# Seven block products for eight in half of the K range of 42 pairs of transposed units, with the attention heads kept in DRAM until pooling

## Chip, cores and metric

The kernel runs on one core of one Trainium2 chip. The metric is the time of one execution on the device in microseconds (us); lower is better. TensorE (PE) multiplies, VectorE (DVE) and ScalarE (ACT) work on tiles, GpSimd (POOL) has a few reductions and DMA issues, and SyncE (SP) issues nearly all DMAs.

## The reference

The input `x` is 512 rows of 2048 float32 values. Two layers follow each other. Each norms its rows, multiplies them with a wide input matrix, mixes the columns, and multiplies 2048 mixed columns with an output matrix:

```python
def even_mixer(h, w_in, pool_w, pool_scale, w_out, cos, sin):
    z = h @ w_in                                   # 1024 a_in, 1024 a_gate, 3 x 3072 q k v, 1024 b_gate
    a_in, a_gate, q, k, v, b_gate = jnp.split(z, _split_points(EVEN_COLS), axis=-1)
    ya = causal_pool_mixer(a_in, pool_w, pool_scale) * jax.nn.silu(a_gate)
    yb = dilated_attention(q, k, v, cos, sin) * jax.nn.silu(b_gate)
    return jnp.concatenate([ya, yb], axis=-1) @ w_out

def odd_mixer(h, w_in, ...):
    z = h @ w_in                                   # six groups of 1024 columns
    u, v, c_gate, d_val, d_glu, d_gate = jnp.split(z, _split_points(ODD_COLS), axis=-1)
    yc = chunked_sgu(u, v, ...) * jax.nn.silu(c_gate)
    d = d_val * jax.nn.sigmoid(d_glu)
    d = jax.nn.silu(layernorm(causal_depthwise_conv(d, ...), ...))
    yd = d * jax.nn.silu(d_gate)
    return jnp.concatenate([yc, yd], axis=-1) @ w_out
```

Attention has eight heads of 128 columns, each the softmax mixture of three dilated groups, with rotation of the first 32 columns of q and k.

## The kernel before

The normed rows stand transposed in SBUF in two parts, `Ah` and `Al` (128 partitions, 16 K tiles of 128, 512 tokens each), whose sum is the float32 value. A weight chunk is 128 x 1024 float32, 512 KB. SP loads it into `wraw` (three buffers); ACT copies it into the high part `whi` (L64), DVE takes the rest into the low part `wlo` (L65); there are three buffers of each part. Every product of a weight tile and a K tile is three matmuls: low weights with `Ah`, high weights with `Al`, high weights with `Ah`.

A *transposed unit* (`zt_item`, L125) makes 128 output columns for all 512 tokens in one PSUM bank: two chunks of 8 K tiles, 48 matmuls of 128x512 (L137 to L139). A *natural item* (`nat_item`, L146) makes rows of tokens by columns (L162 to L164), with 512 columns too; V, both output projections and the odd layer's V are of this kind.

The order of the even layer is: V for heads 0 to 3, 28 units (per head q and k of three groups, and the gate), V for heads 4 to 7, 28 units, then 16 pooling units with two small products (`mix_item`), then the output projection. The odd layer has four natural items, 24 units for the convolution's and the SGU's inputs (with the convolution's taps on DVE beside them, L681), 16 gate units, and the output projection.

When a head's last unit is done, `attention` (L430) starts: scores on PE (L445, L457), maximum over the groups (a POOL reduction, L474), subtraction (L479 to L483), exp on ACT (L481, L484), sums (L468 to L472), a second POOL reduction, a reciprocal (L503), while PE multiplies the exps with V (`oa`, `ob`, L490 to L497); two products (L504, L505) leave the gated head in `Y[:, 8 + h]`. A scheduler that follows the program's order fixes the order on each engine; engines then run their own lists in order and wait on semaphores. Pooling takes its tiles `xp`, `pa`, `pb` from the memory that the attention's tiles leave free (L569, L573).

Of the kernel before, what the change touches and what calls it, by code (L numbers as in the profile page):

```python
# [19 lines left out]
P = 128  # L20
D = 2048
# [13 lines left out]
P_END = 64 + 8 * TAPS  # L35


class Weights:
    """Streams the weight chunks in the order of use and splits each into two float32r parts."""

    def __init__(self, nc, raw_pool, split_pool, chunks, raw_bufs, ahead):
        self.nc, self.raw_pool, self.split_pool, self.chunks = nc, raw_pool, split_pool, chunks
        self.raw_bufs, self.ahead = raw_bufs, ahead
        self.raw, self.parts = [], []
# [12 lines left out]
    def split(self, upto):  # L57
        while len(self.parts) < min(upto, len(self.chunks)):
            i = len(self.parts)
            self.load(i + 1)  # L60
            hi = self.split_pool.tile([P, 1024], FR, tag="whi", name=f"whi{i}")
            lo = self.split_pool.tile([P, 1024], FR, tag="wlo", name=f"wlo{i}")
            for c in ((slice(0, 512), slice(512, 1024)) if i == 0 else (slice(0, 1024),)):
                self.nc.scalar.activation(hi[:, c], self.raw[i][:, c], AF.Copy)  # L64
                self.nc.vector.tensor_tensor(lo[:, c], self.raw[i][:, c], hi[:, c].bitcast(F32), op=OP.subtract)  # L65
            self.parts.append((hi, lo))

    def get(self, i):
        self.split(i + 1)
        self.load(i + 1 + self.raw_bufs)  # L70
        self.split(i + 1 + self.ahead)
        self.load(i + 1 + self.ahead + self.raw_bufs)
        return self.parts[i]


@with_exitstack
def trunk(ctx: ExitStack, tc: tile.TileContext, x, xt, out, ewv, ewz, ewo, epw, epost,
# [4 lines left out]
    raw_pool = ctx.enter_context(tc.tile_pool(name="raw_pool", bufs=3))  # L82
    split_pool = ctx.enter_context(tc.tile_pool(name="split_pool", bufs=3))
    xpool = ctx.enter_context(tc.tile_pool(name="xpool", bufs=2))
    small = ctx.enter_context(tc.tile_pool(name="small", bufs=2))
    dpool = ctx.enter_context(tc.tile_pool(name="dpool", bufs=1, space=bass.MemoryType.DRAM))
    psz = ctx.enter_context(tc.tile_pool(name="psz", bufs=4, space=bass.MemoryType.PSUM))
# [9 lines left out]
    x1d = dpool.tile([S, D], F32, name="x1d")  # L97

# [12 lines left out]

    def rsqrt_of(ssq, n, name):
# [7 lines left out]
    items = []  # L120

    def add_item(chunks, pe, after=None):
        items.append((chunks, pe, after))

    def zt_item(wz, u, after, order=(0, 1), mid=None):  # L125
        state = {}

        def pe(ci, hi, lo):
# [11 lines left out]
            if mid is not None:  # L140
                mid(ci)

        add_item([wz[u, :, 8 * o:8 * o + 8, :].rearrange("p k c -> p (k c)") for o in order], pe,
                 lambda: after(state["ps"]))

    def nat_item(wv, c, tts, after, perm=False, order=range(8), stagger=False):  # L146
# [36 lines left out]
        add_item([wv[c, :, 2 * o:2 * o + 2, :].rearrange("p k c -> p (k c)") for o in order], pe)  # L183
# [17 lines left out]
    def run_items(w, pos):  # L201
        for chunks, pe, after in items:
            for ci in range(len(chunks)):
                hi, lo = w.get(pos)
                pe(ci, hi, lo)
                done.append(pos)
                pos += 1
                if after is not None and ci == len(chunks) - 1:
                    after()
                step()  # L210
        items.clear()
        return pos

# [22 lines left out]
    first = {}  # L236

    def first_loads(i, t, chunk):
# [13 lines left out]
        if 2 <= i <= 5:  # L252
            xr = xpool.tile([P, D], F32, tag="xr", name=f"xn{i}")
# [32 lines left out]

    def load_rows(half, layer, rows):
        src = x if layer == 0 else x1d
        for tt in (2 * half, 2 * half + 1):
            if layer == 1 and half == 1:  # L290
                xr = od["V"][:, 2 * (tt - 2):2 * (tt - 1), :].rearrange("p a b -> p (a b)")
            else:
                xr = xpool.tile([P, D], F32, tag="xr", name=f"xr{layer}_{tt}")
# [87 lines left out]
    # ================= start =================  # L381
# [8 lines left out]
    # ================= even layer, attention =================  # L390
# [19 lines left out]

    def qk_after(g, qk, key):
        def after(ps):
            t = att.tile([P, S], F32, tag="qk", name=f"qk_{len(done)}", bufs=8)
            cos, sin = rp[:, 0, :], rp[:, 1, :]
            sw = att.tile([32, S], F32, tag="sw", name=f"sw_{len(done)}")
            if g == 0:
                nc.scalar.activation(t, ps, AF.Copy)
# [3 lines left out]
            else:  # L421
                nc.scalar.activation(perm_out(t), perm_in(ps), AF.Copy)  # L422
# [4 lines left out]
            qk[key] = t  # L427
        return after

    def attention(h, qk):  # L430
# [67 lines left out]
        y = Y[:, 8 + h, :]  # L498
# [6 lines left out]
        nc.vector.tensor_tensor(y, y, oas, op=OP.mult)  # L505
        yield 1

    def bgate_after(h, qk):
        def after(ps):
            nc.scalar.activation(Y[:, 8 + h, :], ps, AF.Silu)  # L510
            start(attention(h, qk))
        return after

    chunk_list = []
    w = Weights(nc, raw_pool, split_pool, chunk_list, 3, 2)
# [381 lines left out]
```

## Time and profile before

| | before |
|---|---|
| median of 3 runs | 2072.93 us (2072.93 to 2073.49) |
| the profiled execution: span from first to last instruction | 2071.4 us |
| PE busy, share of the span | 2055.5 us, 99% |
| DVE busy | 1156.7 us, 56% |
| ACT busy | 647.1 us, 31% |
| DMA, mean over the span | 117 GB/s |

The span leaves out what comes before the first and after the last instruction, so 1.5 us lie around it. A busy PE need not be a PE at its peak: matmuls are pipelined, so the distance from the start of one to the start of the next is the price of one, and the length of its record is not.

### The profile page before, as it was taken

How to read it: one execution, taken by the hardware profiler on the slowest of the kernel's cores; microseconds unless marked ns; L12 is line 12 of the kernel's file. 1: busy time of each engine (PE TensorE's matmuls, PEld its weight loads, DVE VectorE, ACT ScalarE, POOL GpSimd, SP SyncE). 2: the span in 40 equal slices, each digit the busy share in tenths (PEclk: the TensorE clock that was granted, in tenths of full speed). 3: DMA queues.
4: the chain of work that ended last, by engine and by line, in shares of the span. 5: the costliest groups of instructions: out<-in, count | busy, mean ns of one | idle time of the engine just before them, and what ended most of it. 6: DMA issues, size and time to landing. Idle time of an engine off the chain costs nothing.

```text
span 2071.4 us, 22339 instructions
## 1 busy us (share of the span) xinstructions
PE 2055.5 (99%) x9064; PEld 1699.7 (82%) x9064; DVE 1156.7 (56%) x1385; ACT 647.1 (31%) x793; POOL 87.4 (4%) x86
## 2 busy tenths in 40 slices
PE   8999999999999999999999999999999999999998
PEld 8988888889988888888888888888888888888886
DVE  4725656555224656566542435775889996324255
ACT  6422222323222322223332324553122223323243
POOL 1000101000000101001000000100000001000002
PEclk9999999999999999999999999999999999999999
DMA  8332222232322222222223337864222222223465
GB/s 299 92 101 89 94 83 82 86 98 82 92 92 92 89 85 91 82 92 82 92 93 101 112 97 222 281 216 155 87 92 92 97 97 92 92 91 122 133 211 196
DMA packets 68472, 241.78 MB, mean 117 GB/s; under 512 B 7792, under 2 KB 8048, under 8 KB 67088
## 3 DMA queue, kind: packets, MB, share of 16 engines
q1 hardware_dynamic: 67152, 234.05, 35.0%
q0 software_dynamic: 1216, 6.29, 0.8%
q8 instruction: 71, 1.16, 0.2%
q14 instruction: 33, 0.27, 0.0%
HBM read 231.93 MB, written 8.39 MB: 116 GB/s over the span
## 4 chain that ended last, share of the span: by engine, by line
PE 97%; DMA 1%; DVE 1%; ACT 0%; issue 0%; POOL 0%; SPq 0%; DVEq 0%; ACTq 0%; POOLq 0%
PE z L138 20%; PE z L137 20%; PE z L139 20%; PE n L162 11%; PE n L163 11%; PE n L164 11%; PE sg L457 1%; DMA wraw<-in_owv_dram 0%; DVE Y L313 0%; PE ob L497 0%; PE ob L496 0%; PE oa L490 0%; PE sgu L640 0%; PE sa L445 0%; PE tr L222 0%; DMA wraw<-in_owo_dram 0%
## 5 line engine op out<-in xcount | busy, mean ns | idle before, releaser
L65 DVE TENSOR_TENSOR wlo<-wraw,whi 128x1024 fp32r<-128x1024 f32 (+1 forms) x403 | 504.1, 1251 | 571.3 <-ACT whi L64 570.6
L137 PE MATMUL z<-Ah,wlo 128*128 128x512 f32 x1792 | 710.5, 396 | 0.0
L138 PE MATMUL z<-Al,whi 128*128 128x512 f32 x1792 | 708.8, 396 | 0.0
L64 ACT ACTIVATE whi<-wraw 128x1024 fp32r<-128x1024 f32 (+1 forms) x403 | 425.5, 1056 | 906.9 <-PE z L139 463.8
L139 PE MATMUL z<-Ah,whi 128*128 128x512 f32 x1792 | 708.7, 395 | 0.0
L163 PE MATMUL n<-wlo,Ah 128*128 128x512 f32 x1024 | 406.8, 397 | 0.3 <-DVE wlo L65 0.2
L164 PE MATMUL n<-whi,Ah 128*128 128x512 f32 x1024 | 405.5, 397 | 0.0
L139 PEld LDWEIGHTS z<-Ah,whi 128*128 128x128 f32 x1792 | 336.6, 188 | 81.0
L137 PEld LDWEIGHTS z<-Ah,wlo 128*128 128x128 f32 x1792 | 336.7, 188 | 80.6
L138 PEld LDWEIGHTS z<-Al,whi 128*128 128x128 f32 x1792 | 336.7, 188 | 80.6
L162 PE MATMUL n<-whi,Al 128*128 128x512 f32 x1024 | 392.3, 398 | 6.7 <-DVE Al L263 6.7
L162 PEld LDWEIGHTS n<-whi,Al 128*128 128x128 f32 x1024 | 223.2, 218 | 41.6 <-DVE Al L263 6.7
L163 PEld LDWEIGHTS n<-wlo,Ah 128*128 128x128 f32 x1024 | 223.4, 218 | 36.3 <-DVE wlo L65 1.3
L164 PEld LDWEIGHTS n<-whi,Ah 128*128 128x128 f32 x1024 | 223.3, 218 | 35.0
L681 DVE SCALAR_TENSOR_TENSOR Y<-dp,pc,Y 128x512 f32<-128x512 f32 x240 | 174.3, 749 | 3.6
L423 DVE LOAD_MASK_SELECT sw<-qk x32 | 0.4, 14 | 125.4 <-ACT qk L422 125.4
L422 ACT ACTIVATE qk<-z 128x512 f32<-128x512 f32 x32 | 19.1, 597 | 145.3 <-PE z L139 145.3
L474 POOL PARTITION_ALL_REDUCE mw<-mv x8 | 14.3, 1784 | 798.9 <-DVE mv L472 798.9
L424 DVE TENSOR_TENSOR sw<-sw,rp 32x512 f32<-32x512 f32 x32 | 34.3, 1071 | 1.1
L425 DVE TENSOR_TENSOR qk<-qk,rp 32x512 f32<-32x512 f32 x32 | 34.0, 1063 | 0.0
L426 DVE TENSOR_TENSOR qk<-qk,sw 32x512 f32<-32x512 f32 x48 | 32.3, 673 | 0.2
L735 DVE TENSOR_TENSOR Y<-Y,og 128x512 f32<-128x512 f32 x16 | 11.1, 691 | 38.0 <-ACT og L734 38.0
(153 smaller groups left out, 908.1 us busy)
## 6 DMA issues: line engine op xcount, KB each, us to landing
wraw<-in_ewz_dram SPq DMA_DIRECT2D x144, 512.0 KB, 3.7
wraw<-in_owz_dram SPq DMA_DIRECT2D x80, 512.0 KB, 3.8
wraw<-in_ewo_dram SPq DMA_DIRECT2D x48, 512.0 KB, 4.2
wraw<-in_owo_dram SPq DMA_DIRECT2D x48, 512.0 KB, 3.9
wraw<-in_ewv_dram SPq DMA_DIRECT2D x47, 512.0 KB, 3.6
wraw<-in_owv_dram SPq DMA_DIRECT2D x32, 512.0 KB, 3.8
xn<-in_x_dram SPq DMA_DIRECT2D x4, 1024.0 KB, 8.7
xr<-in_x_dram SPq DMA_DIRECT2D x16, 256.0 KB, 5.1
```

What stands on the lines that cost most here:

```text
L64: self.nc.scalar.activation(hi[:, c], self.raw[i][:, c], AF.Copy)
L65: self.nc.vector.tensor_tensor(lo[:, c], self.raw[i][:, c], hi[:, c].bitcast(F32), op=OP.subtract)
L137: nc.tensor.matmul(ps, wl[:, j], Ah[:, k, :], start=first, stop=False)
L138: nc.tensor.matmul(ps, wh[:, j], Al[:, k, :], start=False, stop=False)
L139: nc.tensor.matmul(ps, wh[:, j], Ah[:, k, :], start=False, stop=last)
L162: nc.tensor.matmul(ps, tok(Al, k, t), wh[:, j], start=first, stop=False)
L163: nc.tensor.matmul(ps, tok(Ah, k, t), wl[:, j], start=False, stop=False)
L164: state["mm"] = nc.tensor.matmul(ps, tok(Ah, k, t), wh[:, j], start=False, stop=last).ins
L424: nc.vector.tensor_tensor(perm_out(sw), perm_out(sw), perm_in(sin), op=OP.mult)
L425: nc.vector.tensor_tensor(perm_out(t[0:32, :]), perm_out(t[0:32, :]), perm_in(cos), op=OP.mult)
L426: nc.vector.tensor_tensor(t[0:32, :], t[0:32, :], sw, op=OP.add)
L681: nc.vector.scalar_tensor_tensor(acc, dp[:, k:k + S], wk, acc, op0=OP.mult, op1=OP.add)
```

## The change

For 42 pairs (u, v) of units (24 pairs of q and k, 4 of two heads' gates, 7 of pooling units, 7 of odd gate units) K tiles 0 to 7 are multiplied as before. For K tiles 8 to 15 the weights of both units and the activations are taken as 2 x 2 blocks: weights by unit and by half of the K range (tiles 8 to 11, and 12 to 15), activations by half of the K range and by half of the tokens. The eight block products of the plain form become seven (a Strassen form), each 4 K tiles by 256 tokens by three matmuls, 12 matmuls of 128x256. The sums of weight blocks are made on DVE in the raw buffers (L78) and then split (L69, L70); the sums of activation blocks, `S1` to `S4`, are made once per layer by `make_forms` (L191, L195). The sums of results are made by ACT copies of 256 columns out of PSUM (L294) and DVE additions (L297, L330) into a destination in SBUF.

Weights now have four raw and four split buffers. Part i of the split weights is made only once part i-4 has been used up, and raw load i only once raw buffer i-4 is released; the first weight chunk of a pair is released by the pair's last part. A head's gated result goes to DRAM (`ybd`, L741, a DMA from POOL's queue), and is read back into `Y` before pooling (L1067, on SP's queue). The scheduler's order follows from all this.

```diff
+RAW_BUFS, SPLIT_BUFS = 4, 4
...
+    def pair(self, ap, bp):
+        a, b = self.chunk(ap), self.chunk(bp)
+        L, R = slice(0, 512), slice(512, 1024)
+        def tt(out, x, y):
+            self.nc.vector.tensor_tensor(out, x, y, op=OP.subtract)
+        def f0(hi, lo):
+            self.split(hi, lo, self.raw[a])
+        def f1(hi, lo):
+            ra, rb = self.raw[a], self.raw[b]
+            tt(ra[:, L], rb[:, L], ra[:, L])
+            self.split(hi[:, L], lo[:, L], ra[:, L])
+            self.split(hi[:, R], lo[:, R], rb[:, R])
+        def f2(hi, lo):
+            ra, rb = self.raw[a], self.raw[b]
+            tt(rb[:, L], rb[:, R], rb[:, L])
+            tt(rb[:, R], rb[:, R], ra[:, L])
+            tt(ra[:, R], ra[:, R], rb[:, R])
+            self.split(hi, lo, rb)
+        def f3(hi, lo):
+            self.split(hi[:, L], lo[:, L], self.raw[a][:, R])
+        return [(self.part, ([a], f0, [])), (self.part, ([a, b], f1, [])),
+                (self.part, ([b], f2, [b])), (self.part, ([a], f3, [a]))]
     def load(self, upto):
         while len(self.raw) < min(upto, len(self.chunks)):
             i = len(self.raw)
+            if i >= self.raw_bufs and not self.raw_done[i - self.raw_bufs]:
+                return
...
+    def pump(self):
+        while True:
+            self.load(len(self.chunks))
             i = len(self.parts)
-            self.load(i + 1)
+            if i == len(self.specs) or (i >= self.split_bufs and not self.done[i - self.split_bufs]):
+                return
+            needs, make, frees = self.specs[i]
+            if any(r >= len(self.raw) for r in needs):
+                return
             hi = self.split_pool.tile([P, 1024], FR, tag="whi", name=f"whi{i}")
             lo = self.split_pool.tile([P, 1024], FR, tag="wlo", name=f"wlo{i}")
-            for c in ((slice(0, 512), slice(512, 1024)) if i == 0 else (slice(0, 1024),)):
-                self.nc.scalar.activation(hi[:, c], self.raw[i][:, c], AF.Copy)
-                self.nc.vector.tensor_tensor(lo[:, c], self.raw[i][:, c], hi[:, c].bitcast(F32), op=OP.subtract)
+            make(hi, lo)
+            for r in frees:
+                self.raw_done[r] = True
...
+    ybd = dpool.tile([8, P, S], F32, name="ybd")
...
+    def make_forms(layer, full, temps):
+        for i, n in enumerate(("S1", "S2", "S3", "S4")):
+            t = rpool.tile([P, 2, 4, 256], FR, tag=f"r{i}", name=f"{n}_{layer}")
+            FORMS[n] = (t[:, 0], t[:, 1])
...
+        for half in range(2):
+            ta, tb, tc_ = temps
+            a21, a22 = full(2, 1, half, ta), full(2, 2, half, tb)
+            tt(tb, a21, a22, OP.add)
+            split("S1", tb, half)
+            a11 = full(1, 1, half, tc_)
+            tt(ta, a11, a21, OP.subtract)
+            split("S3", ta, half)
+            yield 1
+            tt(tb, tb, a11, OP.subtract)
+            split("S2", tb, half)
+            a12 = full(1, 2, half, tc_)
+            tt(tc_, a12, tb, OP.subtract)
+            split("S4", tc_, half)
...
+    def pair_item(wz, u, v, dst_u, dst_v, after_u, after_v):
+        st = {}
+        ZL, XL = slice(0, 256), slice(256, 512)
+        L, Rt = slice(0, 512), slice(512, 1024)
+        makers = w.pair(chunk_of(wz, u, 1), chunk_of(wz, v, 1))
+        def made(i):
+            f, args = makers[i]
+            return f(*args)
+        def product(bank, where, hi, lo, name, start=False):
+            fh, fl = FORMS[name]
+            wh = hi.rearrange("p (k c) -> p k c", c=P)
+            wl = lo.rearrange("p (k c) -> p k c", c=P)
+            out = st[bank][:, where]
+            for j in range(4):
+                nc.tensor.matmul(out, wl[:, j], fh[:, j, :], start=start and j == 0, stop=False, skip_group_check=True)
+                nc.tensor.matmul(out, wh[:, j], fl[:, j, :], start=False, stop=False, skip_group_check=True)
+                nc.tensor.matmul(out, wh[:, j], fh[:, j, :], start=False, stop=j == 3, skip_group_check=True)
...
+        def s0(hi, lo):
+            st["a"] = zbank(f"a_{len(done)}")
+            st["u"], st["v"] = dst_u(), dst_v()
+            product("a", XL, hi[:, L], lo[:, L], "A11", start=True)
+            product("a", ZL, hi[:, Rt], lo[:, Rt], "A12")
+            copy(st["u"][0], "a", XL)
+        def s1(hi, lo):
+            st["b"] = zbank(f"b_{len(done)}")
+            product("b", ZL, hi[:, L], lo[:, L], "S1", start=True)
+            copy(st["u"][1], "b", ZL)
+        def s2(hi, lo):
+            direct("a", hi, lo, range(8))
+            add(st["u"][0], "a", ZL)
+            copy(st["u"][1], "a", XL)
+            after_u()
+        def s3(hi, lo):
+            product("a", XL, hi[:, Rt], lo[:, Rt], "S2")
+            copy(st["v"][0], "a", XL)
+        def s3b(hi, lo):
+            product("b", ZL, hi[:, Rt], lo[:, Rt], "S4")
+        def s4(hi, lo):
+            direct("b", hi, lo, range(3))
+        def s5(hi, lo):
+            product("a", XL, hi[:, L], lo[:, L], "S3")
+            copy(st["v"][1], "a", XL)
+            nc.vector.tensor_tensor(st["v"][1], st["v"][1], st["u"][1], op=OP.add)
+        def s6(hi, lo):
+            direct("b", hi, lo, range(3, 8))
+            add(st["v"][0], "b", ZL)
+            add(st["v"][1], "b", XL)
+            after_v()
+        def s7(hi, lo):
+            product("a", XL, hi[:, L], lo[:, L], "A22")
+        stage(made(0), s0, step=False)
+        p1 = made(1)
+        stage(p1, s1, free=False)
+        flush()
+        p3 = made(2)
+        stage(p3, s3, free=False, step=False)
+        stage(p1, s3b, step=False)
+        p4 = w.plain(chunk_of(wz, v, 0))
+        stage(p4, s4, free=False)
+        stage(p3, s5, step=False)
+        stage(p4, s6)
+        stage(made(3), s7, step=False)
+        tail.append(lambda: (w.plain(chunk_of(wz, u, 0)), s2, True, None, True))
...
-        y = Y[:, 8 + h, :]
+        y = gates[h]
...
         nc.vector.tensor_tensor(y, y, oas, op=OP.mult)
+        nc.gpsimd.dma_start(ybd[h], y)
...
-                for i, (g, key) in enumerate((g, key) for g in range(3) for key in "qk"):
-                    zt_item(ewz, 7 * h + i, qk_after(g, qk, f"{key}{g}"))
-                zt_item(ewz, 7 * h + 6, bgate_after(h, qk))
+                for g in range(3):
+                    def last(h=h, qk=qk, rotate=qk_after(g, qk, f"q{g}")):
+                        rotate()
+                        attend(h, qk)
+                    pair_item(ewz, 7 * h + 2 * g, 7 * h + 2 * g + 1, qk_dst(g, qk, f"q{g}"), qk_dst(g, qk, f"k{g}"),
+                              last if g == 2 else qk_after(g, qk, f"q{g}"), qk_after(g, qk, f"k{g}"))
+                if h % 2 == 0:
+                    pair_item(ewz, 7 * h + 13, 7 * h + 6, bgate_dst(h + 1), bgate_dst(h),
+                              bgate_after(h + 1), bgate_after(h))
...
+        work = Y[:, 4:8, :].rearrange("p a b -> p (a b)")
+        mix["pa"], mix["pb"], mix["t"] = work[:, 0:528], work[:, 528:1056], work[:, 1056:1568]
+        mix["xp"] = [mp.tile([P, 16 + S], F32, name=f"xp{i}") for i in range(4)]
+        mix["n"] = 0
+        for t in mix["xp"] + [mix["pa"], mix["pb"]]:
+            nc.gpsimd.memset(t[:, 0:16], 0.0)
+        for h in range(8):
+            nc.sync.dma_start(Y[:, 8 + h, :], ybd[h])
+        run_section(1)
```

Three places show what this does to the order on the engines. Names with `S_0_785` are the activation sums, `a_7657` and `b_7693` the two banks of the first pooling pair. The first place is PE at the end of attention, around the last head. Before, it reads:

```order
L457 MATMUL sg_2_5969<-qk_5815,qk_5883 128x128 [waits DVE_49,Activation_49]
L457 MATMUL sg_2_5969<-qk_5815,qk_5883 128x128 x3
L137 MATMUL z_6035<-Ah,wlo_5891 128x512 [waits PE_49]
...
L137 MATMUL z_6035<-Ah,wlo_5922 128x512 [waits DVE_49]
...
L137 MATMUL z_6106<-Ah,wlo_6030 128x512 [waits DVE_49,PE_49]
...
L490 MATMUL oa_5995<-sa_5952,Y 128x128 [waits PE_49,Activation_49]
```

Between the last scores `sg_2` and the products `oa` with the exps stand a whole pooling unit (`z_6035`, 48 matmuls) and 16 matmuls of the next. In the changed kernel the same place reads:

```order
L278 MATMUL b_7693<-S_0_784,whi_7506 128x256
L692 MATMUL sg_2_7580<-Y 128x128 [waits DVE_49,Activation_49]
L692 MATMUL sg_2_7580<-Y 128x128 x3
L725 MATMUL oa_7610<-sa_7563,Y 128x128 [waits Activation_49]
...
L731 MATMUL ob_7618<-sg_7564,V_98 128x128 [waits Activation_49]
...
L732 MATMUL ob_7618<-sg_7564,Y 128x128
L276 MATMUL a_7657<-S_0_785,wlo_7526 128x256 [waits Activation_49]
```

Now `oa` comes straight behind the scores, and behind `ob` stands a product of the first pooling pair that waits for ACT. That ACT instruction is the copy `xp<-a` in the second place, ACT's list at the same point:

```order
L716 ACTIVATE sa_7563<-sa_7563 128x896 [waits DVE_49]
L719 ACTIVATE sg_7564<-sg_7564 128x1024 [waits DVE_49]
L735 ACTIVATE o_7627<-oa_7610 128x512 [waits DVE_49,PE_49,Pool_49]
L294 ACTIVATE xp_7639<-a_7657 128x256 [waits DMASW4_49,DMASW5_49,DVE_49,DMASW6_49,PE_49,DMASW7_49,Activation_49,Pool_49]
L294 ACTIVATE xp_7639<-b_7693 128x256
```

The copy waits for four DMA semaphores of the software queue (`DMASW`), which the writes `ybd<-y` of the last heads set, since `xp` lies where the heads' tiles lay. Before, the copy in its place waited for no DMA:

```order
L484 ACTIVATE sg_5953<-sg_5953 128x1024 [waits DVE_49]
L64 ACTIVATE whi_6100<-wraw_5925 128x1024 [waits DMAHW7_49,PE_49,Activation_49]
L500 ACTIVATE o_6012<-oa_5995 128x512 [waits DVE_49,PE_49,Pool_49]
L64 ACTIVATE whi_6131<-wraw_6033 128x1024 [waits DMAHW0_49,PE_49,Activation_49]
L569 ACTIVATE xp<-z_6035 128x512 [waits DVE_49,Activation_49,Pool_49]
```

The third place is DVE in one pair of q and k of a strided group. Here is the changed kernel, from the low part of the pair's first chunk to the low part of the first chunk of the unit before (`wlo_3009`), which PE takes after the pair's first three products:

```order
L70 TENSOR_TENSOR wlo_2953<-wraw_2944,whi_2952 128x1024 [waits DMAHW2_49,Activation_49]
L78 TENSOR_TENSOR wraw_2944<-wraw_2946,wraw_2944 128x512 [waits DMAHW3_49,DVE_49]
L78 TENSOR_TENSOR wraw_2946<-wraw_2946 128x512 [waits DVE_49]
L330 TENSOR_TENSOR Y<-Y 128x64x4 [waits Activation_49]
L70 TENSOR_TENSOR wlo_2980<-wraw_2944,whi_2979 128x512 [waits PE_49,Activation_49]
L70 TENSOR_TENSOR wlo_2980<-wraw_2946,whi_2979 128x512 [waits Activation_49]
L78 TENSOR_TENSOR wraw_2946<-wraw_2946,wraw_2944 128x512 [waits DVE_49]
L297 TENSOR_TENSOR Y<-Y,b_2866 128x64x4 [waits PE_49]
L297 TENSOR_TENSOR Y<-Y,b_2866 128x64x4
L78 TENSOR_TENSOR wraw_2944<-wraw_2944,wraw_2946 128x512 [waits DVE_49]
L70 TENSOR_TENSOR wlo_3009<-wraw_2948,whi_3008 128x1024 [waits DMAHW4_49,Activation_49]
```

Before, the chunks' low parts alternated with the rotation of one unit:

```order
L65 TENSOR_TENSOR wlo_4011<-wraw_3909,whi_4010 128x1024 [waits DMAHW1_49,PE_49,Activation_49]
L426 TENSOR_TENSOR qk_4003<-qk_4003,sw_4004 32x512 [waits DVE_49]
L65 TENSOR_TENSOR wlo_4042<-wraw_3946,whi_4041 128x1024 [waits DMAHW2_49,Activation_49]
L423 STREAM_SHUFFLE sw_4072<-qk_4071 32x512 [waits DVE_49,Activation_49]
L424 TENSOR_TENSOR sw_4072<-sw_4072,rp 32x512 [waits DVE_49]
L425 TENSOR_TENSOR qk_4071<-qk_4071,rp 32x512
L65 TENSOR_TENSOR wlo_4079<-wraw_3977,whi_4078 128x1024 [waits DMAHW3_49,PE_49,Activation_49]
```

Between two neighbouring low parts stood at most three short instructions; now nine stand between `wlo_2953` and `wlo_3009`, four of them the subtractions of L78.

## Rows read from the trace of the kernel before

**Rows 1.** The page: span, busy time and instructions by engine, the chain by engine

```profile
span 2071.4 us, 22339 instructions
PE 2055.5 (99%) x9064; PEld 1699.7 (82%) x9064; DVE 1156.7 (56%) x1385; ACT 647.1 (31%) x793; POOL 87.4 (4%) x86
PE 97%; DMA 1%; DVE 1%; ACT 0%; issue 0%; POOL 0%; SPq 0%; DVEq 0%; ACTq 0%; POOLq 0%
```

**Rows 2.** Timeline of PE in a V item: start us, duration us, instruction

```profile
599.76 0.39 PE L163 MATMUL n<-wlo,Ah 128*128 128x512 f32 x1
599.99 0.40 PE L164 MATMUL n<-whi,Ah 128*128 128x512 f32 x1
600.23 0.39 PE L162 MATMUL n<-whi,Al 128*128 128x512 f32 x1
```

**Rows 3.** Timeline of PE at its first matmuls

```profile
8.57 0.63 PE L163 MATMUL n<-wlo,Ah 128*128 128x512 f32 x1
9.00 0.63 PE L164 MATMUL n<-whi,Ah 128*128 128x512 f32 x1
```

**Rows 4.** Timeline of PE: scores of head 7 (two records for each float32 matmul)

```profile
953.33 1.02 PE L445 MATMUL sa<-qk,qk 128*128 128x256 f32 x4
954.85 1.95 PE L457 MATMUL sg<-qk,qk 128*128 128x128 f32 x16
```

**Rows 5.** Groups of DVE by line and form: count, busy us, mean ns, idle before

```profile
L65 DVE TENSOR_TENSOR wlo<-wraw,whi 128x1024 fp32r<-128x1024 f32 x401 | 502.7, 1254 | 566.4 <-ACT whi L64 565.6
L424 DVE TENSOR_TENSOR sw<-sw,rp 32x512 f32<-32x512 f32 x32 | 34.3, 1071 | 1.1
L228 DVE SCALAR_TENSOR_TENSOR Al<-tr,pc,Ah 128x256 fp32r<-128x256 f32 x32 | 13.3, 475 | 0.2 <-ACT Ah L227 0.2
L419 DVE TENSOR_TENSOR sw<-sw,rp 32x512 f32<-32x512 f32 x16 | 10.8, 674 | 0.1
L479 DVE TENSOR_TENSOR sa<-sa,mw 128x512 f32<-128x512 f32 x8 | 5.5, 684 | 0.0
```

**Rows 6.** Groups of ACT by line and form, the same columns

```profile
L64 ACT ACTIVATE whi<-wraw 128x1024 fp32r<-128x1024 f32 x401 | 424.2, 1058 | 904.5 <-PE z L139 463.8 <-PE n L164 361.2 <-issue 51.7
L339 ACT ACTIVATE Ah<-Y 128x512 fp32r<-128x512 f32 x32 | 18.4, 624 | 2.3 <-DVE Y L735 0.9 <-DVE Y L591 0.9
```

**Rows 7.** DMA issues: count, KB each, median us from issue to landing

```profile
wraw<-in_ewz_dram SPq DMA_DIRECT2D x144, 512.0 KB, 3.7
out_dram<-Y POOLq DMA_DIRECT2D x8, 256.0 KB, 4.3
```

**Rows 8.** Busy by stretch: us, PE, PEld, DVE, ACT, POOL, clock, DMA share, GB/s

```profile
270.00:520.00 250.00, 250.00 (x1147) 211.68 (x1146) 146.89 (x174) 67.37 (x74) 15.64 (x6) 1.00 0.28 88
2064.00:2071.00 7.00, 0.00 (x0) 0.00 (x0) 3.22 (x4) 0.72 (x1) 2.18 (x2) 0.77 0.56 207
```

**Rows 9.** Timeline of DVE: head 7 from its scores to its end

```profile
958.04 0.69 DVE L468 TENSOR_TENSOR mu<-sg 128x512 f32<-128x512 f32 x1
959.89 0.56 DVE L472 TENSOR_TENSOR mv<-mv,sa 128x384 f32<-128x384 f32 x1
...
965.74 2.08 DVE L483 TENSOR_TENSOR sg<-sg,mw 128x512 f32<-128x512 f32 x2
968.95 0.69 DVE L468 TENSOR_TENSOR du<-sg 128x512 f32<-128x512 f32 x1 [1.13 <-ACT sg L484]
...
976.18 3.33 DVE L503 RECIPROCAL dw<-dw 128x512 f32<-128x512 f32 x1
...
981.22 0.69 DVE L505 TENSOR_TENSOR Y<-Y,o 128x512 f32<-128x512 f32 x1
```

**Rows 10.** Timeline of POOL in the same stretch

```profile
960.62 1.78 POOL L474 PARTITION_ALL_REDUCE mw<-mv  x1 [67.89 <-DVE mv L472]
972.54 3.23 POOL L474 PARTITION_ALL_REDUCE dw<-dv  x1 [10.14 <-DVE dv L472]
```

**Rows 11.** Timeline of ACT in the same stretch

```profile
982.03 0.60 ACT L569 ACTIVATE xp<-z 128x512 f32<-128x512 f32 x1 [3.95 <-DVE Y L505]
```

More of the change, by code (lines that the diff above doesn't have):

```diff
@@ L117, in rsqrt_of, with stage, flush, chunk_of @@
         return r
-    items = []
-    def add_item(chunks, pe, after=None):
-        items.append((chunks, pe, after))
+    w = Weights(nc, raw_pool, split_pool, RAW_BUFS, SPLIT_BUFS)
+    program = []
+    stages = []
+    tail = []
+    def stage(part, pe, free=True, after=None, step=True):
+        stages.append((part, pe, free, after, step))
+    def flush():
+        if tail:
+            stages.append(tail.pop()())
+    def chunk_of(wz, u, o):
+        return wz[u, :, 8 * o:8 * o + 8, :].rearrange("p k c -> p (k c)")
     def zt_item(wz, u, after, order=(0, 1), mid=None):
@@ L181, in pe @@
                             run(late, *h)
-        add_item([wv[c, :, 2 * o:2 * o + 2, :].rearrange("p k c -> p (k c)") for o in order], pe)
+        flush()
+        for ci, o in enumerate(order):
+            stage(w.plain(wv[c, :, 2 * o:2 * o + 2, :].rearrange("p k c -> p (k c)")),
+                  lambda hi, lo, ci=ci: pe(ci, hi, lo), free=not stagger or ci < 5)
     done = []
@@ L199, in start, with section, run_section @@
         background.append([gen, 0])
[L201 to L209, printed above, removed]
+    def section(build):
+        build()
+        flush()
+        program.append(list(stages))
+        stages.clear()
+    def run_section(n):
+        for part, pe, free, after, stepping in program[n]:
+            hi, lo = w.get(part)
+            pe(hi, lo)
+            done.append(part)
+            if free:
+                w.free(part)
+            if after is not None:
+                after()
+            if stepping:
                 step()
-        items.clear()
-        return pos
+            w.pump()
     def to_A(half, pcol0):
@@ L285, in norm_first, with full @@
                 yield 1
+        def full(i, k, half, t):
+            k0 = 4 + 4 * k + 2 * half
+            return Y[:, k0:k0 + 2, 256 * i - 256:256 * i]
+        temps = [att.tile([P, S], F32, tag="tmp", name=f"sum{n}", bufs=3).rearrange("p (k t) -> p k t", k=2)
+                 for n in range(3)]
+        yield from make_forms(0, full, temps)
     def load_rows(half, layer, rows):
@@ L505, in attention, with bgate_dst, dst, bgate_after @@
         nc.vector.tensor_tensor(y, y, oas, op=OP.mult)
+        nc.gpsimd.dma_start(ybd[h], y)
         yield 1
[L508 to L511, printed above, removed]
-        return after
-    chunk_list = []
-    w = Weights(nc, raw_pool, split_pool, chunk_list, 3, 2)
-    program = []
-    def section(build):
-        build()
-        program.append(list(items))
-        chunk_list.extend(c for chunks, _, _ in items for c in chunks)
-        items.clear()
-    def run_section(n, pos):
-        items.extend(program[n])
-        return run_items(w, pos)
+    gates, ready = {}, {}
+    def bgate_dst(h):
+        def dst():
+            t = gates[h] = att.tile([P, S], F32, tag="y", name=f"y{h}", bufs=4)
+            return t[:, 0:256], t[:, 256:]
+        return dst
+    def bgate_after(h):
+        def after():
+            nc.scalar.activation(gates[h], gates[h], AF.Silu)
+            attend(h)
+        return after
+    def attend(h, qk=None):
+        ready.setdefault(h, []).append(qk)
+        if len(ready[h]) == 2:
+            start(attention(h, [q for q in ready[h] if q is not None][0], gates))
     def build_attention():
@@ L738, in gate_after, with pgate_dst, dst, pgate_after @@
         return after
+    def pgate_dst(j):
+        def dst():
+            t = od[f"g{j}"] = od["V"][:, j % 4, S:]
+            return t[:, 0:256], t[:, 256:]
+        return dst
+    def pgate_after(j):
+        def after():
+            t = od[f"g{j}"]
+            nc.scalar.activation(t, t, AF.Silu)
+            nc.vector.tensor_tensor(Y[:, j, :], Y[:, j, :], t, op=OP.mult)
+        return after
+    def odd_full(i, k, half, t):
+        h, l = (A[:, 2 * half:2 * half + 2, :] for A in block(i, k))
+        nc.vector.tensor_tensor(t, h.bitcast(F32), l.bitcast(F32), op=OP.add)
+        return t
     def build_odd():
@@ L744, in u_item, with after @@
         def u_item(j):
-            zt_item(owz, 16 + j, u_after(j))
+            def after(ps):
+                u_after(j)(ps)
+                if j == 5:
+                    start(make_forms(1, odd_full, [od["V"][:, n, S:].rearrange("p (k t) -> p k t", k=2)
+                                                       for n in range(3)]))
+            zt_item(owz, 16 + j, after)
         for j in range(8):
```

181 lines of the change are left out of this document (121 added, 60 removed).

## The prediction

> **What bounds the kernel now.** I read the page first, then PE's timeline, then the groups and the timelines of the other engines. The page shows PE busy 2055.5 of 2071.4 us, and a chain of waits that is 97% PE [rows 1]: almost nothing is gained or lost except through what PE does or waits for. Its timeline prices a product: matmuls of 128x512 start 0.23 and 0.24 us apart, 0.47 for two, so about 0.2335 each [rows 2], whatever the 0.39 of the record. A unit of 96 such matmuls for two (48 each) costs 22.4 us. DVE and ACT feed PE; DVE is busy 146.9 of 250 us in a stretch of attention [rows 8], and spends 566 us waiting for ACT's high parts [rows 5], which in turn wait for PE to free a buffer [rows 6]. So the weights run ahead of PE, and their latency costs nothing today.
>
> **Part 1, PE's saving.** Per pair, 48 matmuls of 512 columns (K tiles 8 to 15 of two units) become 84 of 256. The trace has no such matmul in this number format. From below: a float32 128x128 pass of the scores goes by every (1.95-0.28)/15 = 0.11 us [rows 4], however few columns, and four 128x256 records take (1.02-0.38)/3 = 0.21 for twice the passes. From above: a fixed part. At the first matmuls the distance is 0.43 [rows 3], which is 512/1.2 without rest; at the later 0.2335 it is 512/2.4 = 0.213 and 0.020 over. If 0.020 is a fixed part, 256 columns cost 0.126. If it is a rate (it is absent at the slow level, where a fixed part of that size should show), they cost 0.117. I take 0.117: 84 x 0.117 = 9.8 against 11.2 us, 1.4 us per pair and 58 us over 42 pairs. At 0.112 it is 75 us, at 0.126 25 us; the saving ends at 0.133.
>
> The Trainium skill ("TensorE: Matmul & The Clock Gate", Part 3, The mechanism) says that a weight load overlaps a running matmul only where the row groups differ; and it prices a load of 128 columns at 128/1.2 = 107 ns (LDWEIGHTS). By that, estimated, a full 512-column matmul would cost 320 ns and a 256-column one 213, and the change would lose 2.6 us per pair, 108 us in all. The trace disagrees: 0.2335 [rows 2].
>
> **Part 2, the loop of buffers.** This decides how much of the 58 us stays. The order on the engines ties a pair to the next one: the pair's first weight chunk is released only when its last part is made, and that part waits until PE has finished the second product with part p1. Let PE finish that (the S4 product) at time 0.
> - ACT copies the last part's 512 columns (0.62, [rows 6]), DVE subtracts (0.68, [rows 5]), SP loads the next pair's first chunk into the freed buffer (3.7, [rows 7]), ACT copies 1024 columns (1.06), DVE subtracts (1.25). With 0.3 of hand-overs this is 7.6 us.
> - Meanwhile PE has 24 matmuls of 512 and 12 of 256: 5.6 + 1.4 = 7.0. It stalls 0.6.
> - Then PE has the next pair's first two products and the old pair's last (36 x 0.117 = 4.2), and S1 (1.4): it is through at 13.2. What it wants next is the tail chunk's low part, which stands in DVE's order behind four subtractions, two half splits and three additions [the order above]: 6 x 0.68 + 3 x 0.475 + 1.25 = 6.8 us [rows 5] after 7.6, so 14.4; back to back the ten are some 0.2 shorter.
> - From there PE has 24 of 512 and 24 of 256: 5.6 + 2.8 = 8.4. The period is 22.6 to 22.8 us where I counted 21.0 of PE work, and 22.4 before.
>
> Where the destination is strided (q and k of two groups in three), the three additions read 128x64x4; a strided form costs 1071 against 674 ns at 512 columns [rows 5], so 1.6 times as much, 0.85 us more per pair: period 23.3 to 23.6. So the loop, which nothing held before, gives back all of part 1 in a pair with nothing else on PE.
>
> In attention, four pairs in seven also carry a head's scores or its products with V on PE. The scores take 1.5 us from the first row to the second and 1.9 in it [rows 4], and I put the products at as much: 3.4 each. There PE has 24.4 us of work, and the 2.4 us of latency hide under it. Seven pairs of two heads: before, 7 x 22.4 + 4 x 3.35 = 170.2; after, four laden ones at 24.4, three others at 22.7 to 23.4, and about 1.5 us for softmax work that stands between the parts on DVE: 168.6. Over four such groups I count -6 us. The first pair of each of the four runs finds full buffers and keeps its 1.4 us: -5. Pooling and the odd gates are contiguous, 14 pairs at +0.3 and some more on DVE for windows and gates: +6. Together -5 us, of 58.
>
> **Part 3, the end of attention.** Before, 64 matmuls of a pooling unit stood between the last scores and `oa`, about 15 us [the order above], and the tail of head 7 went by beside them: from `mu` at 958.04 to the last product's end at 981.9, 23.9 us [rows 9], with two POOL reductions of 1.8 and 3.2 and a reciprocal of 3.3 inside [rows 9, 10]; ACT's `xp` copy came at 982.03, after a wait of 3.95 which PE never felt [rows 11]. Now `oa` is next after the scores, and the S2 product behind `ob` waits for ACT's copy into `xp`, which waits for head 7's write to DRAM. From the last scores: about 0.9 until `mu` (masks on DVE), 23.9 less some 2.5 for the three weight splits in between, a write of 4.3 (the only POOL-queue store of that size, [rows 7]), and the copy, 0.3 to 0.6. That makes 27 us; PE has only `oa` and `ob` in it, about 3.4. PE idles about 24 us. It also slows down: in the stretch after PE stopped the granted clock was 0.77 on average [rows 8], so between the levels, and at its start PE ran six matmuls at the lower one [rows 3], a loss of some 1.3 us. I take +25.5, with bounds of +18 (the write lands in 2, and DVE is quicker without splits) and +30.
>
> The Trainium skill ("DMA: Bandwidth & Descriptors", Anatomy of one DMA) gives 2.0 us + bytes/436e3 for a DMA from this queue, an estimate of 2.6 us for 256 KB, and warns that the receipt of a write to DRAM can be long. The row says 4.3; by the page the stall would be 1.7 us shorter.
>
> **Part 4, the rest.** The forms are 32 DVE and 16 ACT instructions per kernel. In the even layer they stand in the first V items, in the odd one among the convolution, where 240 taps keep DVE full but the weights run ahead; I cost them at nothing, and at +5 if their cover is gone. The 4 MB to and from DRAM are small against 117 GB/s for 2071 us. The reads of `ybd` hold SP's queue until the last write; buffers loaded before cover PE.
>
> **Sum.** 2071.4 - 5 + 25.5 = 2092 of span, less about 4 because DVE start-to-start times run under their records in many places of the loop (0.1 us per pair): 2088; with the 1.5 us around the span 2089 us. The profiled execution is, with these, at the median (2072.93), so nothing is shifted.
>
> **Rivals.**
> 1. *The loop does not bind, faster.* If the landing is shorter than 3.7, or the parts on DVE overlap better than their records say, the period falls to PE's 21.0 us and 58 us are kept (75 at 0.112): with the stall of 25.5 that gives 2024 to 2041, and with half of it 2055 to 2069. For it: DVE had 103 of 250 us free [rows 8]. Against: it is a latency of five steps in a row, and free time elsewhere doesn't shorten it. The point where it decides is a mean period of 21.8 us (0.6 x 42 = 25.5).
> 2. *The fixed part, slower still.* At 0.126 each half of the loop's PE work grows too; periods 23 to 24, 42 x 0.5 more: 2105 to 2125. For it: the weight loads are busy 1699.7 us [rows 1], so near the matmuls' own time that little is spare with shorter matmuls.
> 3. *The end of attention is hidden.* If PE's order let other products go ahead, 25 us fall away: 2064. The order shows nothing to put there, so little chance.
> 4. *Balance*: loop gains and stall cancel within 0.2% (4 us, about what a measurement of this kernel tells from no change): 2069 to 2077.
>
> **Chances.** Forecast, slower by 5 to 32 us (2078 to 2105): 0.50. Rival 2 and worse: 0.13. Rivals 1 and 3 (faster): 0.28. Balance: 0.09. The range takes 2045 to 2125, where the loop is half as long or half again as long as I reckon beyond PE's work; the forecast's own is 2078 to 2105. Faster 0.28, same 0.09, slower 0.63.
>
> **What would show it.** PE's start-to-start at the products L276 to L278 near 0.117; a stall of 0.6 to 1.5 us before the next pair's first product, released by DVE's low part L70, and another before the tail chunk; pairs 22.5 to 23.5 us apart in pooling; one idle stretch of some 24 us on PE at the end of attention, ended by ACT's `xp` copy. Pairs 21 us apart, no stall before L276, or a stretch filled by other products would prove me wrong; so would products at 0.126 and more.

## The result and the profile after

The changed kernel takes 2048.08 us (median of 4 runs, 2047.29 to 2048.87) against 2072.93 us (median of 4, 2072.39 to 2073.49): a ratio of 0.9879, 95% interval 0.9865 to 0.9893, so 25 us faster. The prediction said 2089 us and slower. The page of the changed kernel, the same parts as [rows 1]:

```profile
span 2046.6 us, 26314 instructions
PE 2010.9 (98%) x10576; PEld 1747.6 (85%) x10576; DVE 1426.9 (70%) x1887; ACT 786.7 (38%) x1089; POOL 99.9 (5%) x97
PE 97%; DVE 1%; issue 0%; POOL 0%; DMA 0%; ACT 0%; SPq 0%; DVEq 0%; POOLq 0%; ACTq 0%
```

DVE carries 270 us more and PE 45 us less, and the chain of waits that ended last is PE's as before. PE's timeline in the pooling run shows the price that no row of before had (start, duration, instruction):

```profile
984.66 0.40 PE L287 MATMUL b<-Ah,whi 128*128 128x512 f32 x1
984.90 0.28 PE L276 MATMUL a<-S,wlo 128*128 128x256 f32 x1
985.01 0.28 PE L277 MATMUL a<-S,whi 128*128 128x256 f32 x1
...
985.73 0.28 PE L277 MATMUL a<-S,whi 128*128 128x256 f32 x1
```

From 985.01 to 985.73 lie six matmuls of 256 columns: 0.12 us each (0.119 in the mean of 320 between 1000 and 1090 us), and from the first row to the second 0.24 for 512 columns, as in [rows 2]. So 84 cost 10.0 us in place of 11.2 for 48: 1.2 us per pair, 51 us over 42. All of PE's waits, by engine, line and releaser (total us, times, longest):

```profile
PE a L276 <- ACT xp L294: 10.2, 1, 10.2
PE oa L725 <- ACT sa L716: 7.3, 1, 7.3
PE n L371 <- DVE Al L481: 6.4, 1, 6.4
PE sg L692 <- DVE Y L662: 3.3, 1, 3.3
```

The wait of 6.4 is the kernel's start (6.7 in the kernel before). The other three are one place, the end of attention, 20.8 us. There is no wait for a weight's low part (L70) anywhere: the loop of buffers, which by the prediction gives back nearly all of the saving, costs nothing. The tail products of the odd pairs (L285 into bank a) start at 1728.07 and 1749.25, 21.18 us apart, which is PE's own work of 48 x 0.2335 + 84 x 0.119.

At the end of attention the timelines of PE, DVE, POOL and ACT answer to [rows 4 and 9 to 11]: the last scores and four pairs of the products `oa` and `ob`, then the last head on DVE from `mu` on, its write, and the copy into `xp`.

```profile
930.35 2.05 PE L692 MATMUL sg<-Y 128*128 128x128 f32 x8 [3.30 <-DVE Y L662]
...
941.14 0.63 PE L725 MATMUL oa<-sa,Y 128*128 128x128 f32 x2
941.56 0.63 PE L727 MATMUL oa<-sa,Y 128*128 128x128 f32 x2
...
944.51 0.39 PE L732 MATMUL ob<-sg,Y 128*128 128x128 f32 x2
944.73 0.39 PE L731 MATMUL ob<-sg,V 128*128 128x128 f32 x2
```

```profile
933.16 0.69 DVE L703 TENSOR_TENSOR mu<-sg 128x512 f32<-128x512 f32 x1
...
950.95 0.69 DVE L739 TENSOR_TENSOR y<-y,dw 128x512 f32<-128x512 f32 x1
951.68 0.69 DVE L740 TENSOR_TENSOR y<-y,o 128x512 f32<-128x512 f32 x1
```

```profile
952.66 0.56 POOL L741 DMA_DIRECT2D ybd<-y  x1 [5.13 <-DVE y L740]
```

```profile
955.07 0.38 ACT L294 ACTIVATE xp<-a 128x256 f32<-128x256 f32 x1 [10.82 <-DMA ybd<-y]
```

The copy into `xp` is released by the write of the last head, as predicted. PE's rows after it, and busy times and clock of the stretches around it (us, PE, PEld, DVE, ACT, POOL, clock, DMA share, GB/s):

```profile
955.50 0.58 PE L276 MATMUL a<-S,wlo 128*128 128x256 f32 x1 [10.16 <-ACT xp L294]
956.32 0.41 PE L276 MATMUL a<-S,wlo 128*128 128x256 f32 x1
956.96 0.41 PE L276 MATMUL a<-S,wlo 128*128 128x256 f32 x1
```

```profile
926.90:955.50 28.60, 7.84 (x40) 7.24 (x38) 17.49 (x20) 3.78 (x6) 5.71 (x5) 0.62 0.19 64
955.50:965.00 9.50, 9.49 (x48) 9.01 (x49) 2.61 (x3) 2.01 (x5) 0.16 (x2) 0.71 0.08 28
1728.00:1792.00 64.00, 64.00 (x401) 57.45 (x401) 51.63 (x83) 35.02 (x59) 9.87 (x3) 1.00 0.31 97
```

After PE stood, three matmuls take 0.64 us where they take 0.36 otherwise: the lower of TensorE's two levels (256/1.2 = 0.213 us each). In between, two passes of `oa` take 0.42 us, and the last ones of `ob` 0.22. The granted clock is 0.62 over the stretch of the waits, 0.71 over the first 9.5 us of new work, and 1.00 in the pairs.

### The profile page after: what moved, and what is told of

Read it like the earlier page. It is cut to its first block, busy times and chain, and to the rows that moved or that the text cites. A ratio compares the mean times of both kernels' runs of the same rounds, so it can differ in the third digit from the quotient of the medians.

```text
span 2046.6 us, 26314 instructions
## 1 busy us (share of the span) xinstructions
PE 2010.9 (98%) x10576; PEld 1747.6 (85%) x10576; DVE 1426.9 (70%) x1887; ACT 786.7 (38%) x1089; POOL 99.9 (5%) x97
## 4 chain that ended last, share of the span: by engine, by line
PE 97%; DVE 1%; issue 0%; POOL 0%; DMA 0%; ACT 0%; SPq 0%; DVEq 0%; POOLq 0%; ACTq 0%
PE n L371 12%; PE n L373 12%; PE n L372 12%; PE z L251 5%; PE z L249 5%; PE z L250 5%; PE a L276 5%; PE a L278 5%; PE a L277 5%; PE b L285 4%; PE b L287 4%; PE b L286 4%; PE a L285 4%; PE a L286 4%; PE a L287 4%; PE b L277 2%
## 5 line engine op out<-in xcount | busy, mean ns | idle before, releaser
L70 DVE TENSOR_TENSOR wlo<-wraw,whi 128x1024 fp32r<-128x1024 f32 (+1 forms) x529 | 577.8, 1099 | 423.6 <-ACT whi L69 419.9
L69 ACT ACTIVATE whi<-wraw 128x1024 fp32r<-128x1024 f32 (+1 forms) x529 | 499.1, 955 | 842.0 <-PE n L373 350.7
L249 PE MATMUL z<-Ah,wlo 128*128 128x512 f32 x448 | 177.9, 397 | 0.0
L250 PE MATMUL z<-Al,whi 128*128 128x512 f32 x448 | 177.2, 396 | 0.0
L251 PE MATMUL z<-Ah,whi 128*128 128x512 f32 x448 | 177.2, 395 | 0.0
L277 PE MATMUL a<-Al,whi 128*128 128x256 f32 x504 | 141.3, 281 | 0.0
L276 PE MATMUL a<-Ah,wlo 128*128 128x256 f32 x504 | 141.3, 282 | 0.0
L278 PE MATMUL a<-Ah,whi 128*128 128x256 f32 x504 | 141.0, 282 | 0.0
L285 PE MATMUL a<-Ah,wlo 128*128 128x512 f32 x336 | 133.6, 398 | 0.0
L285 PE MATMUL b<-Ah,wlo 128*128 128x512 f32 x336 | 133.2, 396 | 0.0
L286 PE MATMUL a<-Al,whi 128*128 128x512 f32 x336 | 132.9, 395 | 0.0
L287 PE MATMUL a<-Ah,whi 128*128 128x512 f32 x336 | 132.8, 395 | 0.0
L287 PE MATMUL b<-Ah,whi 128*128 128x512 f32 x336 | 132.6, 395 | 0.0
```

The lines of the kernel that those rows point to most:

```text
L69: self.nc.scalar.activation(hi, raw, AF.Copy)
L70: self.nc.vector.tensor_tensor(lo, raw, hi.bitcast(F32), op=OP.subtract)
L249: nc.tensor.matmul(ps, wl[:, j], Ah[:, k, :], start=first, stop=False)
L250: nc.tensor.matmul(ps, wh[:, j], Al[:, k, :], start=False, stop=False)
L276: nc.tensor.matmul(out, wl[:, j], fh[:, j, :], start=start and j == 0, stop=False, skip_group_check=True)
L277: nc.tensor.matmul(out, wh[:, j], fl[:, j, :], start=False, stop=False, skip_group_check=True)
```

## Experiments

**The theories.** A: the loop that the prediction walked through needs buffers that follow each other in a ring. The program's rule (part i after part i-4, load i after raw i-4) only orders the program; the place in memory is another matter: the pool gave out the place that was released first. So the next pair's first load waits for the tail chunk's place, not for the last part of this pair. B: the loop would not bind in a ring either, because its steps overlap better than their records say. For the end of attention, A says that 27 us can be had back there, C that the stall only moves.

### e1: both kinds of buffers in a ring

```diff
-            t = self.raw_pool.tile([P, 1024], F32, tag="wraw", name=f"wraw{i}")
+            t = self.raw_pool.tile([P, 1024], F32, tag=f"wraw{i % 4}", name=f"wraw{i}", bufs=1)
...
-            hi = self.split_pool.tile([P, 1024], FR, tag="whi", name=f"whi{i}")
-            lo = self.split_pool.tile([P, 1024], FR, tag="wlo", name=f"wlo{i}")
+            hi = self.split_pool.tile([P, 1024], FR, tag=f"whi{i % 4}", name=f"whi{i}", bufs=1)
+            lo = self.split_pool.tile([P, 1024], FR, tag=f"wlo{i % 4}", name=f"wlo{i}", bufs=1)
```

> The changed kernel, with each raw and split weight buffer given a fixed place in a ring of four (load i takes the place of load i-4, part i that of part i-4), where the changed kernel lets the pool hand out the place that was released first. Theory A: the loop of buffers that the prediction walked through exists only with such a ring; without it the next pair's first load does not wait for the last part of this pair, and the last part does not wait for the S4 product. With the ring the period of a pair with nothing else on PE should be 22.6 to 23.6 us in place of 21.2, and the whole 2085 to 2100 us. Theory B: the loop would not bind with a ring either, since the landing, the splits and the sums on DVE overlap better than their records say: 2046 to 2052 us, pairs 21.2 us apart.

Measured: 2080.91 us, 1.0038 of before (1.0024 to 1.0052), 33 us slower than the changed kernel. The memory is the same; only the places are fixed. PE's waits now name the low parts:

```profile
PE a L276 <- DVE wlo L70: 8.7, 15, 1.6
...
PE a L285 <- DVE wlo L70: 3.3, 5, 1.3
PE b L276 <- ACT Y L294: 3.2, 4, 1.1
```

The chain that ended last, 97% PE in the changed kernel, is now, by engine:

```profile
PE 72%; DVE 19%; DMA 4%; issue 3%; ACT 2%; POOL 1%; DVEq 0%; SPq 0%; POOLq 0%; ACTq 0%
```

A stretch of this chain in attention (start, duration, what) shows the loop closed: from the low half of one pair's last part over the load, ACT's copy and DVE's list to the next pair's, 22.64 us later. No instruction of PE is in it.

```profile
291.38 0.61 DVE wlo L70
292.01 3.61 DMA wraw<-in_ewz_dram
295.64 1.07 ACT whi L69
296.73 1.23 DVE wlo L70
...
314.02 0.61 DVE wlo L70
314.65 3.60 DMA wraw<-in_ewz_dram
```

B falls. A holds in kind, not in size. The scheduler has spread the scores, so nearly every pair in attention has some of a head's work on PE. Pairs with eight passes of the scores are 22.3 to 23.9 us apart, where their products need 22.1; the others in attention take up to 2 us more than their products. The pooling pairs lose nothing. Three pairs of odd gates lose 1.2, 3.3 and 5.3 us, and there the chain runs through the convolution's layer norm on POOL and DVE (L949 to L978), not through a load. Of the 31 us between the two profiled runs, 20 are there by the end of pooling and the other 10 come in these odd pairs. The total is 4 us under the range.

### e2 and e5: one ring each

e2 has the first of the diff's edits alone, e5 the other two.

> The ring for the raw buffers alone; the split buffers as in the changed kernel. Theory A: the last part is still split at the end of the tail chunk's products, 2.8 us before the S4 product ends, so the next first part is ready 4.8 us after S4 where PE needs it at 7.0, and the tail's low part at 11.6 where PE needs it at 13.2: no stall in contiguous pairs, little in strided ones, 2046 to 2058 us. Theory B: 2046 to 2052 us too, so this run tells nothing between them, but it says which of the two rings binds, if the first run is slow.

> The ring of four for the split buffers alone; the raw buffers as in the changed kernel. Theory A, taken further by the runs with the rings: a stall needs a load that waits for the last part. With the raw buffers handed out in order of release no load does, so this alone should cost little: 2048 to 2056 us. If instead the split buffers alone give most of the 11 us by which both rings are slower than the raw ring, 2057 to 2062 us, and the two waits are independent of each other.

Measured: the raw ring 2070.48 us (0.9988, 0.9979 to 0.9997), 22 us slower than the changed kernel; the split ring 2048.38 us (0.9877, 0.9861 to 0.9894), no different from it. So the raw buffers' places decide, and a ring of split buffers costs 10 us more only when loads are late already. The raw ring alone was expected to cost little; that was wrong. The same odd pair in both kernels shows how the loads move. First the changed kernel: DVE's low parts up to the tail chunk's (the second of the two), SP's load, DVE's low half of the last part, ACT's next copies:

```profile
1788.46 1.82 DVE L70 TENSOR_TENSOR wlo<-wraw,whi 128x512 fp32r<-128x512 f32 x2
```

```profile
1790.31 0.33 SPq L111 DMA_DIRECT2D wraw<-in_owz_dram  x1
```

```profile
1799.13 0.69 DVE L70 TENSOR_TENSOR wlo<-wraw,whi 128x512 fp32r<-128x512 f32 x1 [0.29 <-ACT whi L69]
```

```profile
1801.29 1.06 ACT L69 ACTIVATE whi<-wraw 128x1024 fp32r<-128x1024 f32 x1 [0.98 <-PE b L278]
...
1819.65 0.63 ACT L69 ACTIVATE whi<-wraw 128x512 fp32r<-128x512 f32 x1 [5.26 <-PE a L287]
```

The next pair's first chunk is loaded at 1790.31, when the tail chunk's low part is done (1790.28). The three loads behind it follow in the same way, each 0.03 us after the low part that frees the next place (1793.33, 1794.54, 1799.86). The high part of the first chunk is made at 1801.29, as soon as PE has finished the S4 product (`b L278`), with the load landed at 1794.0. The pair's last part (the 512 wide copy, here of the pair after) is released by the tail products' end (`a L287`), so before S4, not by it. With the raw ring:

```profile
1801.03 0.69 DVE L70 TENSOR_TENSOR wlo<-wraw,whi 128x512 fp32r<-128x512 f32 x1 [0.29 <-ACT whi L69]
```

```profile
1801.75 0.33 SPq L111 DMA_DIRECT2D wraw<-in_owz_dram  x1
```

```profile
1807.60 1.06 ACT L69 ACTIVATE whi<-wraw 128x1024 fp32r<-128x1024 f32 x1 [5.11 <-DMA wraw<-in_owz_dram]
```

Now the load goes out as the last part's low half ends (1801.72), and ACT waits for its landing until 1807.60: the chain of the prediction, 5.8 us from issue to use where it had 3.7. In the changed kernel the load starts 9.5 us before the last part's low half ends. In this pair the late load still costs PE nothing (21.25 us to the next pair); in attention, where DVE rotates q and k as well, it reaches PE. (The scheduler also orders instructions otherwise in the ring kernels, on DVE above all, and no run parts this from the places. With the raw ring 15 of the 23 us between the profiled runs come before the end of pooling, with loads in the chain, and 8 in two odd pairs, where the chain goes through the layer norm.)

### e3: plain pairs

```diff
+    def plain_pair(wz, u, v, dst_u, dst_v, after_u, after_v):
+        st = {}
+        for n, key, aft in ((v, "v", after_v), (u, "u", after_u)):
+            def after(ps, key=key, aft=aft):
+                if not st:
+                    st["u"], st["v"] = dst_u(), dst_v()
+                for d, where in zip(st[key], (slice(0, 256), slice(256, 512))):
+                    p = ps[:, where]
+                    nc.scalar.activation(d, p.rearrange("p (i r) -> p i r", r=4) if len(d.shape) == 3 else p, AF.Copy)
+                aft()
+            zt_item(wz, n, after)
```

with every `pair_item` of the three sections replaced by `plain_pair`.

> The changed kernel with all 42 pairs multiplied in the plain form (48 matmuls of 128x512 for each unit, v first, then u, two ACT copies of 256 columns into the same destinations), the forms still made, heads still written to DRAM. Theory A: a pair costs 22.4 us in place of 21.2, 51 us in all, and the idle stretch at the end of attention stays, about 27 us: 2094 to 2102 us. Theory B: the gain is not from the matmuls but from the four buffers or from the order: 2048 to 2075 us.

Measured: 2072.29 us (0.9995, 0.9986 to 1.0004), not different from before. The time lies in theory B's range, but not for its reason: with the four buffers, the forms and the writes kept and only the products plain, nothing of the gain is left, so the gain is the products'. What theory A had wrong is the stall: PE waits nowhere but at the start, also not at the end of attention (clock 1.00 and no gap from 880 to 1000 us). So neither the writes to DRAM nor the memory of `xp` stall PE by themselves. A plain unit is not copied until its 48 matmuls are through, and there are four banks; a seven-product pair needs its first copy before its fourth product, S2, can start (A11, A12 and S1 come first, and S2 goes into A11's half of the bank). The stall comes from both together.

### e4: xp in the memory of V1

```diff
+    v_stack = ExitStack()
+    vpool = v_stack.enter_context(tc.tile_pool(name="vpool", bufs=1))
+    VX = vpool.tile([P, 4 * (16 + S)], F32, name="VX")
-    V1 = att.tile([P, 4, S], F32, name="V1")
+    V1 = VX[:, 0:4 * S].rearrange("p (a b) -> p a b", a=4)
...
-        mix["xp"] = [mp.tile([P, 16 + S], F32, name=f"xp{i}") for i in range(4)]
+        mix["xp"] = [VX[:, (16 + S) * i:(16 + S) * (i + 1)] for i in range(4)]
...
+    v_stack.close()
```

> The changed kernel with the four xp tiles laid into the memory of V1, which is free once PE has read it for the last head, in place of memory that the whole attention's tiles must leave. The first pooling pair's copies then wait for no write to DRAM. Theory A: the end of attention costs the changed kernel about 27 us (20.8 idle on PE, the rest at the lower clock), and two thirds of it go: 2027 to 2037 us. Theory C: the stall only moves, since the scores, the exps and the sums of the last head follow each other anyway and the weights of the next pair wait behind them: 2043 to 2049 us.

Measured: 2031.17 us (0.9798, 0.9783 to 0.9813), 17 us better than the changed kernel. PE's waits other than the start are 7.1 us (2.4 for the exps, 4.2 for low parts, 0.5 for a copy). C falls.

### e6, e7 and e8: plain pairs first

```diff
-            pair_item(ewz, 56 + j, 57 + j, mix_dst(j, "a"), mix_dst(j + 1, "a"), a_after(j), a_after(j + 1))
+            item = plain_pair if j == 0 else pair_item
+            item(ewz, 56 + j, 57 + j, mix_dst(j, "a"), mix_dst(j + 1, "a"), a_after(j), a_after(j + 1))
```

e6 is this (with a `flush()` ahead of the two units, so that the pair before ends first); e7 has `j < 4`, so two plain pairs; e8 is e6 and e4 together.

> The changed kernel with the first pooling pair in the plain form: its two units write two PSUM banks and need no copy to SBUF before 96 matmuls are through. Theory A: the end of attention stalls because the second product of the first pooling pair goes into a half bank that ACT must have copied first, and the copy waits for the last head's write; two units of 11.2 us are work that waits for nothing, so some 18 of the 27 us go, for 1.2 us of saving given up: 2026 to 2034 us. Theory C (the stall only moves, because the last head's chain holds the weights' splits too): 2042 to 2050 us.

> The first two pooling pairs in the plain form: four units in four banks, 45 us of work without a copy, more than the 28 us of the last head's chain. Theory A: no stall is left on PE at the end of attention and 2.4 us of saving are given up: 2022 to 2027 us. Theory C: as in the run with one plain pair, 2042 to 2050 us.

> The first pooling pair in the plain form and the four xp tiles in the memory of V1. Theory A: the plain pair covers the last head until its products with V, and the copies wait for these and not for the write: no stall of over 2 us is left, one pair's saving is given up: 2021 to 2026 us, the fastest. Theory C: 2031 us as with V1 alone.

Measured: 2034.01 us (0.9809, 0.9795 to 0.9824), 2023.41 us (0.9759, 0.9744 to 0.9773) and 2022.34 us (0.9753, 0.9738 to 0.9767); e6 lies at the upper end of its range, the others within theirs. In e6 one wait is left beside the start:

```profile
PE a L276 <- ACT xp L294: 9.3, 1, 9.3
```

One plain pair covers the last head up to its products with V, not up to its write. With two plain pairs nothing is left but the start; so too in e8:

```profile
PE n L384 <- DVE Al L494: 6.4, 1, 6.4
```

These two tell what the end of attention costs the changed kernel: 2048.1 - 2023.4 is 24.7 us, and 2.4 more for two pairs that gave up their saving, 27 us; by e8 it is 25.7 and 1.2, 27 too. And e3 against e8 tells the saving itself: 2072.3 - 2022.3 is 50 us for 41 pairs, 1.22 us each, as PE's timeline says (to about 1 us in all: the kernel before took 2073.0 us beside e3 and 2073.8 beside e8). e8 beats both kernels; 26 us under the changed one.

## Why the prediction was wrong, point by point

- **Part 1, PE's saving: right, a little large.** Predicted 0.117 us for a matmul of 256 columns and 58 us; measured 0.119 and 51. The fixed part of 0.020 (0.126) is excluded, and so is the price of 0.213 that the prediction named for weight loads that do not overlap.
- **Part 2, the loop of buffers: the step that failed.** The sentence "the pair's first weight chunk is released only when its last part is made", followed by the load "into the freed buffer", took the program's release rule for the place in memory. The rule orders when an instruction is listed; what it waits for on the chip is the last use of the place that it was given, and the pool gave out places in the order in which they came free. The load went to the tail chunk's place, 9.5 us earlier, and the last part to the tail's split place, 2.8 us earlier. So the pairs keep 51 us, where the prediction left them 5 of 58.
  e1 restores the ring, and the kernel is 33 us slower; some 20 of them come with loads in the chain, the other 10 in the odd pairs not. e2 and e5 put the loss on the raw buffers.
- **Its size in a ring** was off too: the contiguous pairs of pooling do not stall (21.2 us, not 22.7), and a load that waits took 3.6 us in e1's loop and 5.8 in e2's pair, where the prediction had 3.7. In e1's loop above PE isn't in the chain at all: DVE's list closes it, with the rotations of q and k in it. That fits pooling pairs without a stall, since they have no rotations, but no run takes DVE's order apart, so this stays open.
- **Part 3, the end of attention: the path right, the size by luck.** Predicted 24 us idle after the scores and 1.3 us of lower clock, 25.5; measured 27, so near only because errors in the parts cancel. After the scores PE is idle for 17.5 us: the head went from `mu` to its last product in 19.2 us (933.16 to 952.37), not 21.4, and the write was quicker. Another 3.3 us, ahead of the scores, which wait for a rotation on DVE (L662), were not foreseen. The other 6 are products at the lower clock, in `sg`, `oa`, `ob` and the first 5 us after. The write took 2.4 us from issue to the copy (952.66 to 955.07), not 4.3; the Trainium skill's figure ("DMA: Bandwidth & Descriptors", Anatomy of one DMA), an estimate of 2.6 us, was nearer. The cause was half told: e3 shows that the wait hurts only because a seven-product pair needs a copy so early.
- **Part 4: nothing speaks against it.** The forms, the reads of `ybd` and the DRAM traffic show nowhere in PE's waits; e3 with all of them is at 0.9995.
- **The sum.** With 51 for the saving, 0 for the loop and 27 for the stall it gives 2072.9 - 51 + 27 = 2049 us; measured 2048.1. Rival 1 was the case that came, with the full saving and the full stall; its times (2024 to 2041 with the stall) were worked out with a saving that the price of 0.119 does not bear, and its reason was not the one found.

## What to carry to other kernels

When several buffers of a pool are released out of order, ask which place the next load is given, not which release the program waits for: with a ring of the same size this kernel took 33 us longer, some 20 of them with late loads in the chain. A block scheme that reads partial results early can make a copy out of PSUM a wait for PE, as at the end of attention here; put work without early copies (the plain units of e6 to e8) where the destination's memory comes free late. And a saving of 1.2 us of 22.4 per pair is kept only where PE is the last to be ready, so look in the waits for the one place where it isn't.

## What the runs showed of the hardware that was not expected

A 128x256 matmul with a weight load of its own starts every 0.119 us, half of the 0.2335 of 512 columns and 0.002 more: the 0.020 us by which 512 columns lie over 512/2.4 are mostly a rate, not a fixed part. After PE's waits at the end of attention the lower clock stayed on for some microseconds of full work: the first 24 products after 955.50 took 5.3 us instead of 2.9, on top of the 20.8 us of waiting.
